# Raw blocks of the output set's two chainless products in eight tiles of the shared pool, and the residual's tiles behind the third group

## The chip, the cores and the metric

The kernel runs on one core of a Trainium2 chip. The metric is the device time of one execution in microseconds. TensorE (PE) multiplies, with its weight loads (PEld) beside it; VectorE (DVE), ScalarE (ACT) and GpSimd (POOL) do the rest of the arithmetic; SyncE (SP) and POOL issue most of the DMA transfers, and ACT a few. Each engine works through its own queue in order. All weights come from HBM in float32 and are used once.

## What is computed

One layer of a decoder trunk on 256 tokens of width 2048: a normalisation, one wide input projection, two token mixers side by side (gated linear attention and differential attention), their branch projections, a gated merge, an output projection, a normalisation and the residual. What matters here is the end:

```python
merged = jax.nn.sigmoid(m_a) * y_a + jax.nn.sigmoid(m_b) * y_b
out = merged @ w_out[l]
x = x + rmsnorm(out, post_norm_g[l])
```

`out` is 256 x 2048. Its columns are worked on in four groups of 512: o0, o1, o2 and o3. `x` on the right is the residual, which is needed only in the very last step.

## The kernel before

**Weights.** Every weight block of 128 x 1024 float32 (0.5 MB) is loaded raw, and then split into a rounded part `hi` (ACT, an `activation` with Copy) and a rest `lo` (DVE, a subtraction), since PE multiplies in a format of less precision: hi with both halves of the activations, lo with one. A unit of a regular group is such a block: twelve matmuls of 512 columns. `schedule()` lays down all units in one list of steps; `take` asks for the next one, and `emit_half` has by then written the load and the split of the four steps after it (`AHEAD`).

**Regular loads** are issued by SP (L311) into tiles tagged "raw", of which there are six. A load waits until the block six places before it in this ring has been split. `hi` and `lo` have three buffers each.

**Sets.** Eight pairs of groups ("sets", numbers 0 to 7) are multiplied as 2 x 2 blocks with seven products in place of eight. The seven products have four units each, of six matmuls (two 512-column halves of one raw block, L698). Set 7, called `OUT`, is the pair o0 and o1 of the output projection; its products come in the order p1, q7, p2, p5, q6, q3, p4. The weight operand of p1, p5, q7, q6 and p4 is a running sum or difference of raw blocks: it is kept in two "chains" of four tiles, to which POOL's accumulating DMAs add the next raw block (L232). A block that goes on the chain this way is a `refill`, issued two steps after the split that read the tile (`late`). The weight operands of **p2 and q3 are single raw blocks, not on a chain** (`chain_of` gives None). For set 7 these eight blocks are loaded by SP into the "raw" ring (L291, tile name raw_s), between the raw_o blocks of group o2.

**The last stretch.** y12 and y13 are the last two groups of the second branch projection (L497; raw_y). Then come the 28 units of set 7, spread between the 8 units of o2 (three or four before each), and then o3. `start_out` loads the chains' first blocks at the step of y12's first unit (`begin_out`). During y13 and set 7 the merged activations are turned: `mh` and `ml` (eight tiles) are the halves of the turned operand, `rawm` (four tiles) its unsplit form, from which `out_sum` makes the sums and `out_split` the pairs `msquare` for the products.

o3 is multiplied twice: once for the first 128 tokens while its blocks arrive, once for the other 128 from the kept splits (`keep`, seven of eight units; L479). Then follow the norm and the residual, and the output is stored (L1380, L1381). The second half of o3 and all that follows it work on blocks that are already split.

**Tiles.** Almost everything of 4 KB per partition lives in one pool of 34 tiles (`u(...)`): the chains, `mh`, `ml`, `rawm`, `msquare`, `keep`, the gains `pg`, the results `yg`, the residual `xres`. A tile is given out in the order in which the program first uses it, as soon as an older one has been read for the last time. `xres` (four tiles, 2 MB) is allocated and loaded by SP right after y13's loop, ahead of the o2 loop (L1349).

**Order.** A scheduler at compile time orders each engine's instructions by readiness and program order; what has no input to wait for, such as a load, moves to the front of its queue as far as its tile is free. Some instructions are pinned with `keep_in_program_order`. The loads of this change aren't.

Of the kernel before, what the change touches and what calls it, by code (L numbers as in the profile page):

```python
# [14 lines left out]
P = 128  # L15
# [114 lines left out]
OUT = 7  # L130
# [27 lines left out]
def chain_of(n, name):  # L158
    if n == OUT:
        return OUT_CHAINS.get(name)  # L160
    chain = PRODUCTS[name][1]
    return chain if chain is None else (chain + n) % 2
# [3 lines left out]
def hybrid_kernel(ctx: ExitStack, tc, xt, xn, preg, postg, w, w2, gkb, glag, lamv, diffg, ident_d, causal_d, lmask_d, out):  # L166
    nc = tc.nc
    pe, act, dve, pool, sp = nc.tensor, nc.scalar, nc.vector, nc.gpsimd, nc.sync
# [10 lines left out]
    def u(shape, name, dtype=F32):  # L179
        count[0] += 1  # L180
        return big.tile(shape, dtype, tag="u", name=f"{name}_{count[0]}")
# [9 lines left out]
    def ps(tag):  # L191
        count[0] += 1
        return psum.tile([P, 512], F32, tag="bank", name=f"{tag}_{count[0]}")
# [19 lines left out]
    chains = [[], []]  # L213
    begin = {steps.index((n, 0)) - 7 for n in (0, 1)}
    begin_out = steps.index(("y12", 0))
    set_steps = [step for step in steps if not isinstance(step[0], str)]

    def piece(key, q):
        size = sizes[key]
        at = begins[key] + q * size * P  # L220
        return w[at : at + P * size].rearrange("(p n) -> p n", p=P)

    refills = []
    plain = {}

    def block(n, name, unit, add=True, which=None):

        chain, (kh, g) = chain_of(n, name), which or PRODUCTS[name][2]
        src = piece(SETS[n][g], 2 * kh + unit // 2)[:, 1024 * (unit % 2) : 1024 * (unit % 2) + 1024]
        dst = chains[chain][unit] if chain is not None else plain[n, unit]  # L230
        if add:
            return pool.dma_start(dst, src, accum_op=ALU.add)  # L232
        return pool.dma_start(dst, src)  # L233

    def refill(i, n, name, unit, raw):

        late = lambda *args, **kw: refills.append((i + 2, args, kw))
        x, y = chains[n % 2][unit], chains[(n + 1) % 2][unit]
        if n == OUT:
            if name == "p1":  # L240
                late(n, "p5", unit)
            elif name == "q7":
                late(n, "q6", unit, which=(0, 0))
            elif name == "q6":
                late(n, "p4", unit)
        elif name == "p1":
            if n < 2:
                block(n, "q3", unit, add=False)
            late(n, "p5", unit)
        elif name == "p5" and n in MOVED:  # L250
            late(n, "q6", unit)
        elif name == "p5":
            dve.tensor_tensor(out=x, in0=x, in1=y, op=ALU.add)
            late(n, "q7", unit)
        elif name == "p2" and n in MOVED:
            late(n, "q7", unit)
        elif name == "p2":
            tc.keep_in_program_order(dve.tensor_tensor(out=x, in0=x, in1=raw, op=ALU.add))
        elif name == "q6" and n in MOVED:
            late(n, "p4", unit)  # L260
        elif name == "q6" and n not in FULL:
            plain[n, unit] = u([P, 1024], "plain")
            late(n, "p2", unit, add=False)
        elif name == "q7" and 0 < n < LAST:
            late(n + 1, "p1", unit, add=False)
        elif name == "p4" and 0 < n < LAST:
            late(n + 1, "q3", unit, add=False)
        while refills and refills[0][0] <= i:
            _, args, kw = refills.pop(0)
            block(*args, **kw)  # L270

    def emit_half():
        j = emitted[0]
        emitted[0] += 1
        key, unit = steps[j]
        if j in begin:
            start_sets()
        if j == begin_out:
            start_out()
        if isinstance(key, int):  # L280
            i = set_steps.index((key, unit))
            name, part = order_of(key)[unit // 4], unit % 4
            if key == 1 and part == 0 and unit < 16:
                fetch_square(PRODUCTS[order_of(key)[unit // 4 + 1]][0])
            chain, (kh, g) = chain_of(key, name), PRODUCTS[name][2]
            if (key, part) in plain and name == "p2":
                raw = plain.pop((key, part))
            elif chain is None:
                raw = wpool.tile([P, 1024], F32, tag="raw", name=f"raw_s{key}_{unit}", bufs=6)
                at = 1024 * (part % 2)  # L290
                sp.dma_start(raw, piece(SETS[key][g], 2 * kh + part // 2)[:, at : at + 1024])  # L291
            else:
                raw = chains[chain][part]
            hi_t = wpool.tile([P, 1024], F32R, tag="hi", name=f"hi_{j}")
            lo_t = wpool.tile([P, 1024], F32R, tag="lo", name=f"lo_{j}")
            act.activation(hi_t, raw, AF.Copy)  # L296
            dve.tensor_tensor(out=lo_t, in0=raw, in1=f32(hi_t), op=ALU.subtract)  # L297
            refill(i, key, name, part, raw)
            ready[j] = ((key, unit), hi_t, lo_t)
            return  # L300
        size = sizes[key]
        h = unit % 2
        src = piece(key, unit // 2)
        n = size // 2
        early = key == "v0"
        if j == 0:
            load_x(0, 1)
        if j == 2:
            load_x(2, 2)
        raw = wpool.tile([P, 1024], F32, tag="raw", name=f"raw_{key}_{unit}", bufs=6)  # L310
        i = sp.dma_start(raw[:, :n], src[:, n * h : n * h + n])  # L311
        if early:
            tc.keep_in_program_order(i)
            if j == 0:
                load_x(1, 1)
            for kt in X_LOADS[j // 2] if h else ():
                load_x(kt, 4)
        if early:
            prep_x(j)
            if 6 <= j < 14:  # L320
                square_x(j - 6)
        if key == "o3" and j + 1 < len(steps):
            hi_t, lo_t = u([P, 1024], "keep", F32R), u([P, 1024], "keep", F32R)
        else:
            hi_t = wpool.tile([P, 1024], F32R, tag="hi", name=f"hi_{j}")
            lo_t = wpool.tile([P, 1024], F32R, tag="lo", name=f"lo_{j}")
        fine = 2 if j == 0 else 1
        for i in range(fine):
            a, b = n * i // fine, n * (i + 1) // fine
            r = raw[:, a:b]  # L330
            act.activation(hi_t[:, a:b], r, AF.Copy)  # L331
            dve.tensor_tensor(out=lo_t[:, a:b], in0=r, in1=f32(hi_t[:, a:b]), op=ALU.subtract)  # L332
        ready[j] = (key, hi_t, lo_t)
# [325 lines left out]
    def start_sets():  # L659
        n = started[0]  # L660
        started[0] += 1
        while "squares" not in done:
            with tc.issue_after(latest[0]):
                next(operands, None)
        for c in range(2):
            chains[c][:] = [u([P, 1024], f"chain{c}") for _ in range(4)]
        for unit in range(4):
            tc.keep_in_program_order(block(n, "p1", unit, add=False))

    def start_out():  # L670
        for c in range(2):
            chains[c][:] = [u([P, 1024], f"chain{c}") for _ in range(4)]
        for unit in range(4):
            block(OUT, "p1", unit, add=False)
        for unit in range(4):
            block(OUT, "q7", unit, add=False, which=(1, 1))
        for unit in range(4):
            block(OUT, "q7", unit)
# [110 lines left out]
    def late():  # L789
        norm_row()  # L790
        yield
        lam()
        yield
# [102 lines left out]
    for hf in range(2):  # L896
        ts = {}
        for name in ("k", "q"):
            ts[name] = u([P, 2, 4, P], name)
            for c in range(4):  # L900
                o, o2 = (t.rearrange("p (b t) -> p b t", b=2) for t in channel_major(f"{name}{hf}{c}"))
                bc = rstd_bc.rearrange("p (b t) -> p b t", b=2)
                t = ts[name][:, :, c, :]
# [63 lines left out]
    for g in range(4):  # L967
# [5 lines left out]
        t = u([P, 2, 512], "ua")  # L973
# [198 lines left out]
    for g in range(4):  # L1172
# [3 lines left out]
        for b in range(2):  # L1176
            t = t2([P, 512], "part")
# [6 lines left out]
    first, both, raw = {}, {}, {}  # L1184
# [136 lines left out]
    for g in range(4):  # L1321
# [8 lines left out]
        for b in range(2):  # L1330
            t = both[g][:, b, :]
# [9 lines left out]
    pg = [u([P, 1024], "pg") for _ in range(2)]  # L1341
    for i in range(2):
        sp.dma_start(pg[i], postg[1024 * i : 1024 * i + 1024].partition_broadcast(P))
    xres = []
    for b in range(2):
        xres.append([])
        for i in range(2):
            t = u([P, 1024], "xres")
            sp.dma_start(t, xn[P * b : P * b + P, 1024 * i : 1024 * i + 1024])  # L1349
            xres[b].append(t)  # L1350
    yg = [[u([P, 1024], "yg") for _ in range(2)] for _ in range(2)]
    ssq = sm([P, 2, 5], "ossq", bufs=1)

# [4 lines left out]
    def gain(b, bank, lo, n):  # L1358
        c = slice(lo % 1024, lo % 1024 + n)
        dve.tensor_tensor(out=yg[b][lo // 1024][:, c], in0=bank, in1=pg[lo // 1024][:, c], op=ALU.mult)  # L1360
# [22 lines left out]
    for g in (2,):  # L1383
        banks = token_major(f"o{g}", 512, m_ops)
        for b in range(2):
            square(b, banks[b], 512, g)
            gain(b, banks[b], 512 * g, 512)
    bank = ps("mm")
    kept = []
    for q in range(8):  # L1390
# [78 lines left out]
```

## Time and profile before

| | us |
|---|---|
| median of three runs | 1107.38 (1106.74 to 1109.68) |
| the profiled execution | 1108.6 |
| its span in the trace | 1106.8 |
| PE busy | 1089.2 (98%) |
| DVE busy | 891.0 (81%) |
| ACT busy | 723.9 (65%) |
| POOL busy | 195.9 (18%) |
| mean DMA rate | 259 GB/s, 287.17 MB |

The span goes from the first to the last instruction of the trace. Busy time is the time in which an engine had an instruction in work; a matmul's recorded end is modelled, and since matmuls overlap, the distance between the starts of two of them tells more than the length of one: of 512 columns, they start about 0.227 us apart at the full clock. The chain of work that ended last is followed back from the last instruction, at each step to what released it. "Landing" of a transfer is the time from its issue to the arrival of all its bytes. In a group's row, `out<-in` are tile names without buffer numbers.

### The profile page before, as it was taken

To read this page: it belongs to the slowest core of one execution; us is meant where nothing else is said; L and a number is where in the kernel's file an instruction comes from. 1 tells how busy PE (TensorE), PEld (TensorE's weight loads), DVE (VectorE), ACT (ScalarE), POOL (GpSimd) and SP (SyncE) were. 2 spreads that over 40 slices of the span, in tenths; PEclk is the share of its full clock that TensorE was granted. 3 is DMA by queue.
4 is the path that set the end of the run, shared out by engine and by line. 5 is a ranking of instruction groups with operands and counts; after the bars stand their busy time and mean duration, and the time that the engine had idled before them with its cause. 6 is when DMAs were issued, how large, how long until landed. Compare 5 with 4: busy or idle time off the path is not lost.

```text
span 1106.8 us, 15617 instructions
## 1 busy us (share of the span) xinstructions
PE 1089.2 (98%) x5506; PEld 936.4 (85%) x5506; DVE 891.0 (81%) x1233; ACT 723.9 (65%) x1057; POOL 195.9 (18%) x299
## 2 busy tenths in 40 slices
PE   9999999999999999999999999999999999999977
PEld 9999888888888888888888888888888888888866
DVE  6787769997779698879888898887768688688964
ACT  7777455655656668777877777766566565537751
POOL 0112112000311201212221321222111222102100
PEclk9999999999999999999999999999999999999988
DMA  8889775748899758988899978999787999959962
GB/s 310 265 300 335 236 260 209 276 162 279 238 341 273 263 190 231 241 240 246 254 233 255 275 213 262 251 352 307 208 252 239 338 340 327 391 187 254 264 206 76
DMA packets 81966, 287.17 MB, mean 259 GB/s; under 512 B 9888, under 2 KB 10656, under 8 KB 81888
## 3 DMA queue, kind: packets, MB, share of 16 engines
q1 hardware_dynamic: 47792, 164.52, 41.7%
q0 software_dynamic: 33376, 120.60, 41.5%
q10 hardware_dynamic: 720, 1.06, 0.3%
q8 instruction: 43, 0.70, 0.2%
q14 instruction: 35, 0.29, 0.1%
HBM read 262.03 MB, written 24.12 MB: 259 GB/s over the span
## 4 chain that ended last, share of the span: by engine, by line
PE 92%; DVE 3%; DMA 2%; issue 2%; ACT 1%; DVEq 0%; POOLq 0%; POOL 0%; SPq 0%; ACTq 0%
PE mm L497 35%; PE set L698 26%; PE mm L518 15%; PE mm L520 8%; PE bg L497 2%; DMA raw_o<-in_w_dram 1%; PE bg L873 1%; PE bg L479 1%; PE bg L1012 1%; PE bg L1011 1%; DVE lo L297 1%; PE mm L479 0%; DVE lo L332 0%; PE bg L1037 0%; ACT hi L331 0%
## 5 line engine op out<-in xcount | busy, mean ns | idle before, releaser
L297 DVE TENSOR_TENSOR lo<-chain,hi 128x1024 fp32r<-128x1024 f32 x188 | 228.5, 1221 | 66.2 <-ACT hi L296 65.4
L296 ACT ACTIVATE hi<-chain 128x1024 fp32r<-128x1024 f32 x188 | 197.9, 1058 | 124.8 <-PE mm L497 48.8
L518 PE MATMUL mm<-xs,hi 128*128 128x512 f32 x768 | 197.7, 390 | 0.0
L518 PEld LDWEIGHTS mm<-xs,hi 128*128 128x128 f32 x768 | 143.3, 188 | 27.6
L497 PE MATMUL mm<-hi,xs 128*128 128x512 f32 (+2 forms) x640 | 151.7, 377 | 0.9 <-ACT hi L331 0.9
L232 POOL DMA_DIRECT2D chain<-in_w_dram x88 | 76.6, 871 | 358.0 <-DVE lo L297 213.9
L497 PEld LDWEIGHTS mm<-hi,xs 128*128 128x128 f32 x640 | 119.2, 189 | 16.5 <-ACT hi L331 1.2
L698 PE MATMUL set<-hi,square 128*128 128x512 f32 x448 | 121.7, 393 | 0.0
L520 PEld LDWEIGHTS mm<-xs,lo 128*128 128x128 f32 x768 | 104.7, 190 | 8.3 <-DVE lo L332 0.9
L520 PE MATMUL mm<-xs,lo 128*128 128x256 f32 x768 | 107.2, 282 | 0.5 <-DVE lo L332 0.5
L332 DVE TENSOR_TENSOR lo<-raw_y,hi 128x1024 fp32r<-128x1024 f32 x64 | 78.2, 1223 | 31.7 <-ACT hi L331 31.7
L331 ACT ACTIVATE hi<-raw_y 128x1024 fp32r<-128x1024 f32 x64 | 67.9, 1060 | 53.6 <-PE mm L497 34.2
L698 PEld LDWEIGHTS set<-hi,square 128*128 128x128 f32 x448 | 81.6, 189 | 14.6 <-ACT p L715 0.4
L698 PE MATMUL set<-hi,xs 128*128 128x512 f32 x336 | 91.0, 392 | 0.0
L497 PE MATMUL mm<-lo,xs 128*128 128x512 f32 (+2 forms) x320 | 81.9, 374 | 0.0
L698 PEld LDWEIGHTS set<-hi,xs 128*128 128x128 f32 x336 | 61.1, 189 | 10.5
L698 PE MATMUL set<-lo,square 128*128 128x512 f32 x224 | 69.5, 391 | 0.1
L497 PEld LDWEIGHTS mm<-lo,xs 128*128 128x128 f32 x320 | 60.0, 189 | 8.1 <-DVE lo L332 0.3
L233 POOL DMA_DIRECT2D chain<-in_w_dram x64 | 35.5, 571 | 147.0 <-DVE lo L297 114.7
L331 ACT ACTIVATE hi<-raw_ag 128x1024 fp32r<-128x1024 f32 x32 | 34.0, 1061 | 33.2 <-PE mm L497 19.3
L698 PE MATMUL set<-lo,xs 128*128 128x512 f32 x168 | 51.9, 390 | 0.0
L332 DVE TENSOR_TENSOR lo<-raw_v,hi 128x832 fp32r<-128x832 f32 (+2 forms) x41 | 40.9, 1009 | 12.9 <-ACT hi L331 12.8
(309 smaller groups left out, 2095.6 us busy)
## 6 DMA issues: line engine op xcount, KB each, us to landing
chain<-in_w_dram POOLq DMA_DIRECT2D x152, 512.0 KB, 8.8
raw_y<-in_w_dram SPq DMA_DIRECT2D x64, 512.0 KB, 7.0
raw_ag<-in_w_dram SPq DMA_DIRECT2D x32, 512.0 KB, 4.7
raw_dq<-in_w_dram SPq DMA_DIRECT2D x32, 512.0 KB, 6.0
raw_dk<-in_w_dram SPq DMA_DIRECT2D x32, 512.0 KB, 6.1
raw_v<-in_w_dram SPq DMA_DIRECT2D x32, 416.0 KB, 5.8
raw_s<-in_w_dram SPq DMA_DIRECT2D x20, 512.0 KB, 7.7
raw_k<-in_w_dram SPq DMA_DIRECT2D x16, 512.0 KB, 7.0
```

Source lines behind the costliest of these rows:

```text
L232: return pool.dma_start(dst, src, accum_op=ALU.add)
L233: return pool.dma_start(dst, src)
L296: act.activation(hi_t, raw, AF.Copy)
L297: dve.tensor_tensor(out=lo_t, in0=raw, in1=f32(hi_t), op=ALU.subtract)
L331: act.activation(hi_t[:, a:b], r, AF.Copy)
L332: dve.tensor_tensor(out=lo_t[:, a:b], in0=r, in1=f32(hi_t[:, a:b]), op=ALU.subtract)
L479: i = pe.matmul(out, lhs, rhs, start=first and n == 0, stop=last and n == len(pairs) - 1)
L497: i = pe.matmul(banks[g][b][:, :n], a[part][:, P * b : P * b + P], w[:, c : c + n], start=first, stop=last)
L518: i = pe.matmul(o, hi[:, c], x_pair(kt), start=kt == 0, stop=kt == KT - 1)
L520: i = pe.matmul(o[:, :S], lo[:, c], x_ops(kt)[0], start=False, stop=False)
L698: i = pe.matmul(bank, a[part], wt[:, 512 * j : 512 * j + 512], start=go, stop=end, skip_group_check=not first)
L873: pe.matmul(o, xk[:, P * c : P * c + P], xq.rearrange("p (b c t) -> p b c t", b=2, c=4)[:, :, c, :], start=i == 0, stop=i == 1)
```

## The change

For set 7, the eight raw blocks of p2 and q3 no longer go through the "raw" ring. Each has a tile of the shared pool:

- p2's four blocks are allocated and loaded at the step of y13's first unit (`begin_out + 8`), by POOL.
- q3's four blocks are allocated and loaded one by one as p1's four units are split (in `refill`), by SP.
- When the products come, `emit_half` finds the tile in `plain`, which is now keyed by the product's name too, and splits from it. The splits and matmuls are those of before.
- `xres` is allocated and loaded behind the o2 loop rather than ahead of it.

```diff
-    def block(n, name, unit, add=True, which=None):
+    def block(n, name, unit, add=True, which=None, queue=pool):
...
-        dst = chains[chain][unit] if chain is not None else plain[n, unit]
+        dst = chains[chain][unit] if chain is not None else plain[n, name, unit]
         if add:
             return pool.dma_start(dst, src, accum_op=ALU.add)
-        return pool.dma_start(dst, src)
+        return queue.dma_start(dst, src)
...
             if name == "p1":
                 late(n, "p5", unit)
+                plain[n, "q3", unit] = u([P, 1024], "plain")
+                block(n, "q3", unit, add=False, queue=sp)
...
-            plain[n, unit] = u([P, 1024], "plain")
+            plain[n, "p2", unit] = u([P, 1024], "plain")
             late(n, "p2", unit, add=False)
...
+        if j == begin_out + 8:
+            for n in range(4):
+                plain[OUT, "p2", n] = u([P, 1024], "plain")
+                block(OUT, "p2", n, add=False)
...
-            if (key, part) in plain and name == "p2":
-                raw = plain.pop((key, part))
+            if (key, name, part) in plain:
+                raw = plain.pop((key, name, part))
...
     pg = [u([P, 1024], "pg") for _ in range(2)]
     for i in range(2):
         sp.dma_start(pg[i], postg[1024 * i : 1024 * i + 1024].partition_broadcast(P))
-    xres = []
-    for b in range(2):
-        xres.append([])
-        for i in range(2):
-            t = u([P, 1024], "xres")
-            sp.dma_start(t, xn[P * b : P * b + P, 1024 * i : 1024 * i + 1024])
-            xres[b].append(t)
...
     for g in (2,):
         banks = token_major(f"o{g}", 512, m_ops)
         for b in range(2):
             square(b, banks[b], 512, g)
             gain(b, banks[b], 512 * g, 512)
+    xres = []
+    for b in range(2):
+        xres.append([])
+        for i in range(2):
+            t = u([P, 1024], "xres")
+            sp.dma_start(t, xn[P * b : P * b + P, 1024 * i : 1024 * i + 1024])
+            xres[b].append(t)
```

## The prediction, made before the change was run

> **What bounds the kernel now.** First the page: PE is busy throughout, and its slices fall off only at the end, where the change acts.
>
> ```profile
> PE 1089.2 (98%) x5506; PEld 936.4 (85%) x5506; DVE 891.0 (81%) x1233; ACT 723.9 (65%) x1057; POOL 195.9 (18%) x299
> PE   9999999999999999999999999999999999999977
> ```
>
> Next the table of stages over the last 150 us. Its columns are the stretch, its length, busy time of PE, PEld, DVE, ACT and POOL (with instruction counts), granted clock, DMA share, GB/s.
>
> ```profile
> 960.00:980.00 20.00, 20.00 (x90) 16.57 (x89) 16.71 (x15) 8.73 (x10) 0.00 (x0) 1.00 0.75 271
> 980.00:1000.00 20.00, 20.00 (x102) 16.80 (x101) 13.05 (x15) 8.91 (x11) 0.00 (x0) 1.00 0.56 178
> 1000.00:1020.00 20.00, 19.73 (x91) 16.09 (x90) 18.22 (x22) 16.25 (x22) 6.05 (x7) 1.00 0.96 270
> 1020.00:1040.00 20.00, 19.94 (x89) 16.19 (x87) 20.00 (x23) 16.19 (x19) 0.85 (x1) 1.00 1.05 288
> 1040.00:1060.00 20.00, 17.02 (x74) 13.76 (x74) 14.97 (x15) 9.57 (x12) 3.41 (x4) 1.00 0.99 254
> ```
>
> Until 1040 PE loses next to nothing. The DMA engines have room between 960 and 1000 (0.25 x 20 + 0.44 x 20 = 13.8 us) and none from 1000 to 1060. The chain of waits (start, length, what) then names the loss:
>
> ```profile
> 1049.43 11.31 DMA raw_o<-in_w_dram
> ...
> 1060.76 0.04 ACT keep L331
> ...
> 1061.72 1.05 ACT hi L331
> ...
> 1073.64 4.61 DMA raw_o<-in_w_dram
> ...
> 1078.27 1.07 ACT hi L331
> ...
> 1080.51 1.23 DVE keep L332
> ```
>
> A raw block of the last group (o3) takes 11.31 us to land. ACT, which works in order, stands at its split ("keep"); the split that PE needs, of the third group's seventh unit (o2), is queued behind it. PE's timeline prices it (start, length, instruction, idle before):
>
> ```profile
> 1056.40 0.61 PE L698 MATMUL set<-lo,msquare 128*128 128x512 f32 x2
> 1062.81 0.79 PE L497 MATMUL mm<-hi,mh 128*128 128x512 f32 x1 [5.80 <-ACT hi L331]
> 1067.66 0.40 PE L698 MATMUL set<-hi,mh 128*128 128x512 f32 x1
> 1073.13 0.39 PE L497 MATMUL mm<-hi,mh 128*128 128x512 f32 x1
> 1075.85 0.61 PE L479 MATMUL mm<-keep,mh 128*128 128x512 f32 x2
> 1081.29 0.99 PE L479 MATMUL mm<-keep,mh 128*128 128x512 f32 x2
> ```
>
> PE is idle for **5.80 us**. Then one unit (twelve matmuls) takes 1067.66 - 1062.81 = 4.85 us; the same work takes 1075.85 - 1073.13 = 2.72 us later, so **2.13 us** go to a slower clock, which the table in 5 us steps shows:
>
> ```profile
> 1055.00:1060.00 5.00, 2.02 (x9) 1.32 (x8) 0.21 (x1) 0.00 (x0) 0.00 (x0) 1.00 1.03 323
> 1060.00:1065.00 5.00, 2.19 (x5) 1.80 (x6) 2.21 (x2) 3.90 (x4) 0.00 (x0) 0.53 0.55 223
> ```
>
> The Trainium skill ("TensorE: Matmul & The Clock Gate", Part 1: The HAM clock gate) says that an idle window of about 3.4 us halves the clock. The trace agrees: idle from 1057.0, granted clock 0.53 in 1060 to 1065. By that rule a remaining wait below that length would cost itself alone.
>
> At 1081.29 a pair takes 0.99 in place of 0.61: **0.38 us**, again a split queued behind a late load (1073.64). All that the change can win is 5.80 + 2.13 + 0.38 = 8.31 us; PE's other work is untouched.
>
> **The change, part by part.** *The raw ring.* Loads of raw_o and of raw_s (the eight blocks) share six buffers, and a load is issued when the split of the load six places before it is done. SP's timeline (start, time from first to last, line, count):
>
> ```profile
> 999.67 0.33 SPq L291 DMA_DIRECT2D raw_s<-in_w_dram  x1
> ...
> 1001.08 2.58 SPq L1349 DMA_DIRECT2D xres<-in_xn_dram  x4
> ...
> 1028.37 7.81 SPq L291 DMA_DIRECT2D raw_s<-in_w_dram  x3
> 1043.33 30.64 SPq L311 DMA_DIRECT2D raw_o<-in_w_dram  x10
> ```
>
> The change takes eight of the 24 raw loads out of this ring. Then o2's seventh load follows the split of o2's first unit, and o3's first load that of o2's third:
>
> ```profile
> 1009.60 1.21 DVE L332 TENSOR_TENSOR lo<-raw_o,hi 128x1024 fp32r<-128x1024 f32 x1
> ...
> 1024.86 1.22 DVE L332 TENSOR_TENSOR lo<-raw_o,hi 128x1024 fp32r<-128x1024 f32 x1
> ```
>
> So they are issued near 1011 and 1026, not at 1043.33 and 1049.43. o2's fourth to sixth loads move ahead of 1000. That is what removes the 5.80 and the 2.13.
>
> *Price of a load.* 0.524 MB at 420 GB/s is 1.25 us (first row: plain loads). Where accumulating loads of the chains alternate with plain ones, two move in 1.05 MB / 276 GB/s = 3.80 us (second row): about 2.55 us for an accumulating load.
>
> ```profile
> 950.00:955.00 5.00, 5.00 (x24) 4.14 (x23) 3.37 (x3) 2.12 (x2) 2.17 (x5) 1.00 1.03 420
> 1030.00:1035.00 5.00, 5.00 (x24) 4.14 (x23) 5.00 (x6) 4.41 (x7) 0.00 (x0) 1.00 1.06 276
> ```
>
> *p2's four loads* go to POOL. The x tiles are read last at 957.0 (the tile view, first and last start at the row's end), so the pool has tiles then; POOL's next instruction comes only at 1002.67 after 45.27 us of idleness, so four issues (0.54 us each, as for "plain" before) hold up nothing there.
>
> ```profile
> L698 PE MATMUL set<-lo,xs x16: 389/389/389, 928.2 to 957.0; 128*128 128x512 f32 x16
> 1002.67 0.89 POOL L232 DMA_DIRECT2D chain<-in_w_dram  x1 [45.27 <-DVE lo L297]
> L233 POOL DMA_DIRECT2D plain<-in_w_dram x4: 527/542/618, 872.7 to 884.3; - x4
> ```
>
> On the DMA engines they take 4 x 1.25 = 5.0 us beside raw_y's loads. Those issued from 957 to 970 land after (minimum, median, maximum):
>
> ```profile
> DMA to landing us min/median/max: 3.6/6.4/7.1
> ```
>
> A raw_y buffer is needed again after six units of 2.72 us, less about 2.3 us of splitting: some 14 us after its issue. 7.1 + 5.0 = 12.1 fits. Cost 0, from 0 to 1 us if the cover is short.
>
> *q3's four loads* stay on SP, but with tiles of their own, near 975 to 1005 as tiles come free; until then each can hold the raw_y and raw_o loads behind it on SP. The xres loads, in the same position before, waited in total, how often, and longest (us):
>
> ```profile
> SPq L1349 <- PE mm L497: 1.0, 2, 0.6
> ```
>
> The six-deep ring hides that. Cost 0, at most 1 us. With p2's, and o2's three, less the three raw_s loads that already came before 1000, about seven loads, 9 us of DMA time, go into the 13.8 us of room.
>
> *xres* leaves 1001 to 1021 and comes behind o2: four plain loads, 5.0 us, on SP among o3's loads, beside the four accumulating loads of p4 (4 x 2.55 = 10.2 us). p4's issues (first and last start) and their landing (minimum, median, maximum):
>
> ```profile
> L232 POOL DMA_DIRECT2D chain<-in_w_dram x4: 847/851/857, 1041.3 to 1047.0; - x4
> ...
> DMA to landing us min/median/max: 5.5/9.5/13.5
> ```
>
> The last lands at 1060.5 at worst and is split by 1062.8; PE without the stall wants it at 1057.0 + 2.72 + 3 x 1.36 = 1063.8 (a unit of a product is six matmuls, 1.36 us). It fits by 1 us. xres itself is read only from 1089.0:
>
> ```profile
> L1380 DVE SCALAR_TENSOR_TENSOR yg<-yg,or,xres x8: 746/747/753, 1089.0 to 1102.2; 128x512 f32<-128x512 f32 x8
> ```
>
> *Tiles.* The turns write mh in 991.9 to 1018.3:
>
> ```profile
> L530 ACT ACTIVATE mh<-bg x8: 574/586/592, 991.9 to 1018.3; 128x512 fp32r<-128x512 f32 x8
> ```
>
> At the tightest point, near 1016, live are mh and ml 8, chains 8, rawm 4, pg 2, n7's sum and its pair 3, the eight new ones: 33 of 34, and a last gate and part. A wait for a tile there meets the last turn, at 1018, whose sum feeds p5, two products later. I take 0, from 0 to 2 us.
>
> *What is late next* is DVE. Its row for 1020 to 1040 says 20.00 of 20 us. From 1055 it has 14 splits of 1.23 us (the "keep" row above) and six products or sums of 0.67 us
>
> ```profile
> 1077.01 1.33 DVE L1360 TENSOR_TENSOR yg<-mm,pg 128x512 f32<-128x512 f32 x2
> ```
>
> or 21.2 us, ending at 1076.2; PE without the stall needs o3's last split at 1063.8 + 1.36 + 2.72 + 7 x 1.36 = 1077.4. It stays hidden by 1 us.
>
> **Sum.** 8.31 us less 0.4 for the thin margins (1 us at p4's last load and at DVE, the tiles) is 7.9. The profiled execution took 1108.6 us (span 1106.8): 1100.7. It lies 1.2 above the median of the runs, 1107.38; from that, **1099.5 us**.
>
> **Rivals.**
> *(a) xres puts o3's loads late again, in part.* SP and ACT are in order: xres lands behind p4's accumulations, o3's next loads behind xres, and a "keep" split queued too early holds ACT as at 1060.76. For: before, the xres loads landed after
>
> ```profile
> DMA to landing us min/median/max: 8.7/13.5/18.2
> ```
>
> and held the loads behind them. Against: the o3 loads concerned are needed from 1068, not 1057. Price: up to their 5.0 us of DMA time, on average 4: 1101.5 to 1105.5.
>
> *(b) The DMA is the bound, whichever queue.* The Trainium skill ("DMA: Bandwidth & Descriptors", Issuing engines are not separate DMA queues) says that loads from SP, ACT and POOL interleave on the same 16 DMA engines. The trace shows shares of 0.96, 1.05 and 0.99 from 1000 to 1060 with both queues open. If the new loads cannot start before 1000 (tiles come late), o3's last load lands at 1078 as before, and the wait moves to o3: 1107.4 within 2 us. Against: 13.8 us of room and tiles from 957.
>
> *(c) Slower: xres stands ahead of o3's last four loads.* If its tiles come only with the last chain (p4's splits, after 1062), SP waits there, and 5.0 us of xres precede o3's last load: landing 1073.64 + 4.61 + 5.0 = 1083.25. By the chain above PE resumes 3.5 us after that landing (1080.51 + 1.23, against 1078.25), so PE ends 5.0 us later than now: 1112.4. It decides from a last landing later than 1078.25. Against: by my count q3's tiles come free near 1050.
>
> **Chances.** Forecast 0.55 (1097.5 to 1101.5), (a) 0.22, (b) 0.11, (c) 0.12. A measurement tells about 0.3%, 3.3 us, from no change: faster means below 1104.1, slower above 1110.7. Faster 0.55 + 0.16 of (a) = 0.71; same 0.06 + 0.11 = 0.17; slower 0.12. The range takes the forecast, (a), and the nearest of (b): 1097.5 to 1106.0, with 0.8 in it.
>
> **What would show it.** Right: no idle PE near 1057, granted clock 1.00 from 1055 to 1070, raw_o's fourth load before 1000, plain's loads between 957 and 1005, o3's first landing before 1040, DMA share in 960 to 1000 up by 0.2, the tail after o3 unchanged. Wrong: PE waiting for an ACT split whose engine waits for raw_o after 1050 (a), plain's loads after 1000 (b), SP waiting at L1349's successor past 1060 (c), or PE waiting for raw_y near 965.

## The result, and the profile after

| | before | after |
|---|---|---|
| median, measured side by side (6 runs each) | 1107.36 (1106.53 to 1109.68) | 1099.64 (1098.68 to 1100.17) |
| the profiled execution | 1108.6 | 1100.08 |
| its span | 1106.8 | 1098.3 |

The ratio is 0.9926, 95% interval 0.9913 to 0.9939: 7.7 us faster; 1099.64 was measured where 1099.5 was predicted. In the listings of the changed kernel most lines have moved by six: the splits of raw blocks are L337 (ACT) and L338 (DVE), those of chains and of the early blocks L302 and L303, a group's matmuls L503, a set's L704, o3's L485, and SP's raw loads L317. The xres loads, which the change moves, are L1392; the loads of the early blocks ("plain") are L233.

The page after, its two lines on PE:

```profile
PE 1087.1 (99%) x5506; PEld 935.5 (85%) x5506; DVE 891.4 (81%) x1233; ACT 724.1 (66%) x1057; POOL 197.6 (18%) x303
...
PE   9999999999999999999999999999999999999997
```

PE's busy time fell by 2.1 us with the same 5506 matmuls, which is the size of the slow clock's loss; the rest of the 8.5 us of span was idle time. The table of stages, with the columns of the prediction's table:

```profile
960.00:980.00 20.00, 20.00 (x90) 16.57 (x89) 16.44 (x15) 8.99 (x10) 1.81 (x4) 1.00 0.98 392
980.00:1000.00 20.00, 20.00 (x102) 16.82 (x101) 13.05 (x15) 8.91 (x11) 0.00 (x0) 1.00 0.55 180
1000.00:1020.00 20.00, 19.76 (x91) 16.11 (x91) 18.38 (x22) 16.43 (x23) 6.04 (x7) 1.00 0.96 265
1020.00:1040.00 20.00, 20.00 (x89) 16.34 (x88) 20.00 (x23) 15.77 (x19) 0.85 (x1) 1.00 0.95 235
1040.00:1060.00 20.00, 20.00 (x89) 16.48 (x89) 19.72 (x22) 15.36 (x19) 3.41 (x4) 1.00 0.84 184
```

From 1040 to 1060 PE is busy for all 20 us (17.02 before) at clock 1.00, and the DMA share there fell from 0.99 to 0.84. The extra traffic ahead of 1000 shows in the first row alone: (392 - 271) GB/s x 20 us = 2.4 MB, between four and five blocks. PE has one wait left after 940 (who waits for what: us in total, times, longest):

```profile
PE bg L1218 <- DVE mgate L1339: 0.2, 1, 0.2
```

PE's timeline across the place of the old wait (start, length, instruction, idle before in brackets where there is any):

```profile
1056.56 0.62 PE L704 MATMUL set<-lo,msquare 128*128 128x512 f32 x2
1057.02 0.39 PE L503 MATMUL mm<-hi,mh 128*128 128x512 f32 x1
...
1059.73 0.39 PE L704 MATMUL set<-hi,mh 128*128 128x512 f32 x1
...
1067.89 0.61 PE L485 MATMUL mm<-keep,mh 128*128 128x512 f32 x2
```

ACT's timeline, before and then after:

```profile
1060.76 1.06 ACT L331 ACTIVATE keep<-raw_o 128x1024 fp32r<-128x1024 f32 x1 [7.58 <-DMA raw_o<-in_w_dram]
```

```profile
1053.24 1.05 ACT L337 ACTIVATE keep<-raw_o 128x1024 fp32r<-128x1024 f32 x1
1054.19 1.04 ACT L337 ACTIVATE hi<-raw_o 128x1024 fp32r<-128x1024 f32 x1
```

ACT still takes the split of o3's first block ("keep") ahead of that of o2's seventh unit ("hi"), but now the block lies there and neither row has an idle time, where ACT stood 7.58 us before. PE goes from the set to o2's seventh unit without a gap at 1057.02, that unit takes 1059.73 - 1057.02 = 2.71 us, and o3 begins at 1067.89 in place of 1075.85: 7.96 us earlier, against 5.80 + 2.13 = 7.93 in the prediction. From o3's first matmul to the end of the span it is 30.41 us (1098.3 - 1067.89), 0.54 us less than before (1106.8 - 1075.85 = 30.95). SP's timeline:

```profile
983.77 16.50 SPq L317 DMA_DIRECT2D raw_o<-in_w_dram  x6
1000.32 1.52 SPq L233 DMA_DIRECT2D plain<-in_w_dram  x3
1001.95 2.00 SPq L1349 DMA_DIRECT2D pg<-in_postg_dram  x2
1004.04 0.40 SPq L233 DMA_DIRECT2D plain<-in_w_dram  x1
1011.14 54.95 SPq L317 DMA_DIRECT2D raw_o<-in_w_dram  x10
1066.14 1.86 SPq L1392 DMA_DIRECT2D xres<-in_xn_dram  x4
```

o2's first six loads are now all issued by 1000.3. Its seventh follows at 1011.14, and o3's first, the third of the run of ten, in SP's timeline from 1026 to 1027:

```profile
1026.22 0.33 SPq L317 DMA_DIRECT2D raw_o<-in_w_dram  x1
```

These are the 1011 and 1026 of the prediction. o3's first block lands 8.9 us later, at 1035.1, long before ACT comes to it at 1053.24. The xres loads went to the very end, behind all of o3's.

### The profile page after: what moved, and what is told of

It reads as the page before. It is cut to its first block, busy times and chain, and to the rows that moved or that the text cites. A ratio compares the mean times of both kernels' runs of the same rounds, so it can differ in the third digit from the quotient of the medians.

```text
span 1098.3 us, 15622 instructions
## 1 busy us (share of the span) xinstructions
PE 1087.1 (99%) x5506; PEld 935.5 (85%) x5506; DVE 891.4 (81%) x1233; ACT 724.1 (66%) x1057; POOL 197.6 (18%) x303
## 4 chain that ended last, share of the span: by engine, by line
PE 94%; DVE 3%; issue 1%; DMA 0%; ACT 0%; DVEq 0%; POOLq 0%; POOL 0%; SPq 0%; ACTq 0%
PE mm L503 36%; PE set L704 27%; PE mm L524 15%; PE mm L526 8%; PE bg L503 2%; PE mm L485 1%; PE bg L879 1%; PE bg L485 1%; PE bg L1018 1%; PE bg L1017 1%; DVE lo L338 1%; DVE chain L260 1%; PE bg L1043 0%; DVE lo L303 0%; PE bg L1218 0%
## 5 line engine op out<-in xcount | busy, mean ns | idle before, releaser
L303 DVE TENSOR_TENSOR lo<-chain,hi 128x1024 fp32r<-128x1024 f32 x188 | 228.5, 1222 | 65.8 <-ACT hi L302 63.9
L302 ACT ACTIVATE hi<-chain 128x1024 fp32r<-128x1024 f32 x188 | 198.1, 1058 | 125.0 <-PE mm L503 48.9
L503 PE MATMUL mm<-hi,xs 128*128 128x512 f32 (+2 forms) x640 | 151.8, 377 | 0.6 <-ACT hi L337 0.6
L503 PEld LDWEIGHTS mm<-hi,xs 128*128 128x128 f32 x640 | 119.4, 189 | 16.2 <-ACT hi L337 0.9
L704 PE MATMUL set<-hi,square 128*128 128x512 f32 x448 | 121.7, 393 | 0.0
L338 DVE TENSOR_TENSOR lo<-raw_y,hi 128x1024 fp32r<-128x1024 f32 x64 | 78.3, 1223 | 31.7 <-ACT hi L337 31.7
L337 ACT ACTIVATE hi<-raw_y 128x1024 fp32r<-128x1024 f32 x64 | 67.9, 1060 | 53.5 <-PE mm L503 34.1
L704 PEld LDWEIGHTS set<-hi,square 128*128 128x128 f32 x448 | 81.6, 188 | 14.7 <-ACT p L721 0.4
L704 PE MATMUL set<-hi,xs 128*128 128x512 f32 x336 | 91.0, 392 | 0.0
L503 PE MATMUL mm<-lo,xs 128*128 128x512 f32 (+2 forms) x320 | 82.1, 374 | 0.0
L704 PEld LDWEIGHTS set<-hi,xs 128*128 128x128 f32 x336 | 61.1, 189 | 10.5
L704 PE MATMUL set<-lo,square 128*128 128x512 f32 x224 | 69.5, 391 | 0.1
L503 PEld LDWEIGHTS mm<-lo,xs 128*128 128x128 f32 x320 | 60.0, 189 | 8.1 <-DVE lo L338 0.3
L233 POOL DMA_DIRECT2D chain<-in_w_dram x64 | 35.5, 565 | 147.1 <-DVE lo L303 111.8
L337 ACT ACTIVATE hi<-raw_ag 128x1024 fp32r<-128x1024 f32 x32 | 34.0, 1062 | 33.2 <-PE mm L503 19.4
L704 PE MATMUL set<-lo,xs 128*128 128x512 f32 x168 | 51.8, 390 | 0.0
L338 DVE TENSOR_TENSOR lo<-raw_v,hi 128x832 fp32r<-128x832 f32 (+2 forms) x41 | 40.3, 995 | 12.7 <-ACT hi L337 12.5
```

The source lines that it names most:

```text
L233: return queue.dma_start(dst, src)
L503: i = pe.matmul(banks[g][b][:, :n], a[part][:, P * b : P * b + P], w[:, c : c + n], start=first, stop=last)
L704: i = pe.matmul(bank, a[part], wt[:, 512 * j : 512 * j + 512], start=go, stop=end, skip_group_check=not first)
```

## The experiments

The theory was the prediction's: PE waited since ACT, in order, stood at the split of o3's first block, which landed late; and it landed late since its buffer of the ring came free late. The rivals: the full DMA engines bound the stretch whatever the order; and the gain is due to the xres loads leaving it. Each run is compared with runs of the kernel before on the same chip. Line numbers differ by a few from run to run; the tile names tell which instruction it is.

| run | median, us | before, us | ratio (95%) |
|---|---|---|---|
| 1 xres_alone | 1107.40 | 1107.75 | 0.9997 (0.9987 to 1.0006) |
| 2 p2_alone | 1107.41 | 1107.75 | 0.9994 (0.9985 to 1.0004) |
| 3 q3_alone | 1112.83 | 1107.75 | 1.0044 (1.0029 to 1.0059) |
| 4 before_keeps_pinned | 1100.31 | 1107.75 | 0.9933 (0.9917 to 0.9950) |
| 5 both_xres_ahead | 1100.77 | 1107.97 | 0.9933 (0.9918 to 0.9948) |
| 6 q3_last_two | 1105.66 | 1107.97 | 0.9980 (0.9971 to 0.9989) |
| 7 q3_last_one | 1104.63 | 1107.97 | 0.9969 (0.9956 to 0.9981) |
| 8 xres_in_o3 | 1100.11 | 1107.97 | 0.9925 (0.9911 to 0.9938) |
| 9 q3_xres_behind | 1099.97 | 1108.13 | 0.9927 (0.9911 to 0.9943) |
| 10 o3_first_early | 1101.29 | 1108.13 | 0.9937 (0.9923 to 0.9951) |
| 11 after_keeps_pinned | 1098.60 | 1108.13 | 0.9914 (0.9900 to 0.9927) |

**One part at a time (1, 2, 3).** Run 1 is the kernel before with only the xres loads moved behind o2, where the change has them:

```diff
         sp.dma_start(pg[i], postg[1024 * i : 1024 * i + 1024].partition_broadcast(P))
-    xres = []
-    for b in range(2):
...
             gain(b, banks[b], 512 * g, 512)
+    xres = []
+    for b in range(2):
...
```

> The kernel before, with only the residual's loads moved behind the third group. Theory (ring and ACT order): the raw ring still holds all 24 loads, so o3's first load is still issued after the split of o2's sixth unit, near 1049.4, still lands near 1060 and still holds ACT; about 1107.4 us, within 1 us, PE idle 5 to 6 us near 1057. Rival (contention: what counts is how many bytes move between 1000 and 1060): four loads, 5.0 us of DMA time, leave that stretch; about 1103 us.

Run 2 is the kernel before with only p2's four blocks loaded early, by POOL (the lookup in `plain` is that of the change):

```diff
+        if j == begin_out + 8:
+            for n in range(4):
+                plain[OUT, "p2", n] = u([P, 1024], "plain")
+                block(OUT, "p2", n, add=False)
```

> The kernel before, with only p2's four blocks in tiles of the pool, loaded early by POOL; q3 through the ring, the residual ahead of the third group. Theory: the load six places before o3's first is still that of o2's sixth unit, so o3's first load is issued near 1049.4 as before; about 1107.4 us, within 1 us. Rival (contention): one load less after 1000, three raw_o loads earlier; about 1103 to 1105 us.

Run 3 is the kernel before with only q3's four blocks in tiles of their own. xres stays where it was before, as it does in runs 6 and 7, which are variants of this one:

```diff
             if name == "p1":
                 late(n, "p5", unit)
+                plain[n, "q3", unit] = u([P, 1024], "plain")
+                block(n, "q3", unit, add=False, queue=sp)
```

> The kernel before, with only q3's four blocks in tiles of the pool; p2 through the ring, the residual ahead of the third group. Theory: the load six places before o3's first is now that of o2's third unit, split near 1026, so the whole gain is there: 1099.6 us, within 1 us, no idle PE near 1057, granted clock 1.00 from 1055 to 1070. Rival (contention): four loads out of the stretch, the residual still in it; about 1103 us.

For neither xres nor p2 alone is a difference shown. PE's longest wait after 940 in run 1, then in run 2:

```profile
PE mm L497 <- ACT hi L331: 5.0, 1, 5.0
```

```profile
PE mm L501 <- ACT hi L335: 4.9, 1, 4.9
```

The old wait stands in both, a little shorter than the 5.80 us. In run 2 SP's timeline says why four loads fewer in the ring don't help:

```profile
1009.36 0.33 SPq L315 DMA_DIRECT2D raw_o<-in_w_dram  x1
1017.64 17.02 SPq L295 DMA_DIRECT2D raw_s<-in_w_dram  x3
1041.82 29.30 SPq L315 DMA_DIRECT2D raw_o<-in_w_dram  x10
```

The last run of ten begins with o2's last two, and o3's first load is its third. The six places ahead of it are those two, the three raw_s (q3's blocks) and the raw_o of 1009.36. So its buffer comes free with the split of that raw_o, o2's sixth unit, just as in the kernel before. Of the eight blocks only three of q3's stand in between; p2's were never among these six.

Run 3 does take q3's out, and was slower than before, where 1099.6 was expected: a miss. Its waits of PE, then SP's timeline, then the longest transfer of its chain (start, length):

```profile
PE set L700 <- ACT hi L298: 10.1, 1, 10.1
```

```profile
1000.12 1.58 SPq L233 DMA_DIRECT2D plain<-in_w_dram  x3
1001.80 1.03 SPq L1345 DMA_DIRECT2D pg<-in_postg_dram  x2
1002.93 2.46 SPq L1351 DMA_DIRECT2D xres<-in_xn_dram  x4
1006.57 0.33 SPq L233 DMA_DIRECT2D plain<-in_w_dram  x1
1010.94 0.33 SPq L293 DMA_DIRECT2D raw_s<-in_w_dram  x1
```

```profile
1010.94 28.79 DMA raw_s<-in_w_dram
```

The old wait is gone, but q3's four loads (plain), pg's two and xres's four are now one run of ten loads issued on SP within 7 us (a convoy, in what follows), and the next load behind it is p2's last raw block. It lands 28.79 us after its issue, and PE waits 10.1 us for its split. A wait for o3 was exchanged for a longer one for p2. The expectation had also counted wrongly: with p2 still in the ring, six places ahead of o3's first load stands p2's last block, not o2's third unit, so o3's first load was issued at 1042.18, behind that late split, and not near 1026.

**The order on ACT alone (4).** No load is moved; ACT's splits of o3 are held in program order, behind all of o2's and the set's:

```diff
-            act.activation(hi_t[:, a:b], r, AF.Copy)
+            split = act.activation(hi_t[:, a:b], r, AF.Copy)
+            if key == "o3":
+                tc.keep_in_program_order(split)
```

> The kernel before, all loads as they were; only ACT's splits of o3's blocks are pinned in program order, behind the split of o2's eighth unit. Theory: o2's seventh block had landed long before 1057, and the 5.80 us were ACT standing at o3's first block; with the order changed they go, and the slow clock with them, though o3's first load still takes about 11 us: 1099.6 to 1101 us. Rival (the late loads themselves bound the end): 1107 us within 1 us, the wait only moves to o3's first matmul near 1068.

The gain comes whole, as far as the intervals tell. A row of its table of stages, and its ACT timeline:

```profile
1040.00:1060.00 20.00, 20.00 (x90) 16.54 (x89) 19.61 (x20) 13.78 (x17) 3.41 (x4) 1.00 0.99 252
```

```profile
1052.69 1.06 ACT L331 ACTIVATE hi<-raw_o 128x1024 fp32r<-128x1024 f32 x1 [0.70 <-PE set L700]
...
1061.82 2.94 ACT L331 ACTIVATE keep<-raw_o 128x1024 fp32r<-128x1024 f32 x3
```

The DMA engines carry what they carried before (0.99 and 252 GB/s; 0.99 and 254 before), and PE has no wait above 0.3 us after 940: o2's seventh split runs at 1052.69, o3's first at 1061.82, and o3 needs nothing earlier. So the full DMA engines were not the bound, and the late block cost time only through ACT's order: the split of o3's first block stood ahead of one that PE wanted sooner.

**Where xres stands (5, 8).** Run 5 is the changed kernel with the xres loads back ahead of the o2 loop; run 8 is the changed kernel with them pinned between o3's fourth and fifth loads, to bring about what rivals (a) and (c) feared:

```diff
+        if key == "o3" and unit >= 4:
+            tc.keep_in_program_order(i)
...
-            sp.dma_start(t, xn[P * b : P * b + P, 1024 * i : 1024 * i + 1024])
+            tc.keep_in_program_order(sp.dma_start(t, xn[P * b : P * b + P, 1024 * i : 1024 * i + 1024]))
```

> The changed kernel with the residual's loads back ahead of the third group: twelve tiles more in use at once near 1016 than at the end. Theory (ring and ACT order): the ring is as free as in the changed kernel; 1099.6 us within 1 us, waits for tiles hidden. Rival (tiles: the residual had to make room): 37 tiles wanted of 34 near 1016, the last turn waits, PE idle 1 to 4 us between 1010 and 1045; 1101 to 1104 us.

> The changed kernel with the residual's four loads pinned on SP between o3's fourth and fifth load (in the changed kernel they came behind all of o3). Theory: o3's last four loads land up to 5 us later, but PE has the second half of o3's first four units to do meanwhile; 1099.6 us within 1 us. Rival (a) and (c) of the prediction: ACT or PE waits for o3's later blocks; 1101 to 1105 us, PE idle 1 to 5 us after 1068.

No difference from the changed kernel is shown for either. Run 5 lies 1.17 us above the expected 1099.6, just outside its band, with one wait of 0.8 us in o3; PE does not wait near 1016, where the rival feared for tiles. SP's timeline of run 8 from 1040 on:

```profile
1042.30 6.45 SPq L317 DMA_DIRECT2D raw_o<-in_w_dram  x2
1048.80 2.23 SPq L1394 DMA_DIRECT2D xres<-in_xn_dram  x4
1055.36 9.56 SPq L317 DMA_DIRECT2D raw_o<-in_w_dram  x4
```

PE's only wait after 940 in run 8 is one of 0.2 us.

**How many of q3's blocks (6, 7).** The kernel before with only the last two, or the last one, of q3's blocks in tiles of their own:

```diff
+                if unit in (2, 3):
+                    plain[n, "q3", unit] = u([P, 1024], "plain")
+                    block(n, "q3", unit, add=False, queue=sp)
```

> The kernel before, with only the last two of q3's blocks in tiles of the pool. Theory: six places before o3's first load stands o2's fifth unit, split by 1043.4; o3's first load is issued there and lands near 1050, before ACT comes to it near 1053: the whole gain, 1099.6 us within 1 us. Rival (contention): half of q3's share, about 1105 us.

> The kernel before, with only the last of q3's blocks in a tile of the pool. Theory: six places before o3's first load stands q3's first block, split by 1048.0; o3's first load is issued 1.4 us earlier than before and lands near 1058, so PE idles about 3 us near 1057 and not 5.8. If so short a pause leaves the clock at 1.00, the time is about 1102.6 us; if the clock still drops, about 1104.7 us. Rival (contention): an eighth of the loads, about 1106 us.

Run 6 missed for the reason of run 3, by a convoy of eight: PE waits 3.45 us for the split of p2's last block. In run 7 PE does not wait for p2's block, and the old wait is only shortened, to 3.05 us, since o3's first load follows a block one place earlier. The clock stayed at 1.00, for which 1102.6 had been expected; that 1104.63 agrees with the 1104.7 expected for a dropped clock is chance. What the expectation left out are further waits of PE for DVE, 0.7 us in o3 and 0.5 us at the set. PE's row at each wait, with the clock around it:

```profile
1034.03 0.80 PE L701 MATMUL set<-hi,mh 128*128 128x512 f32 x1 [3.45 <-ACT hi L299]
```

```profile
1030.00:1035.00 5.00, 1.55 (x5) 0.99 (x4) 1.34 (x2) 2.08 (x3) 0.00 (x0) 0.86 1.07 278
1035.00:1040.00 5.00, 5.00 (x19) 4.05 (x18) 4.52 (x5) 4.86 (x7) 0.00 (x0) 0.80 1.03 311
```

```profile
1058.99 0.50 PE L500 MATMUL mm<-hi,mh 128*128 128x512 f32 x1 [3.05 <-ACT hi L334]
```

```profile
1055.00:1060.00 5.00, 1.95 (x9) 1.29 (x8) 1.03 (x1) 3.07 (x4) 0.00 (x0) 1.00 1.01 338
1060.00:1065.00 5.00, 5.00 (x23) 4.11 (x22) 5.00 (x7) 3.88 (x6) 0.00 (x0) 1.00 0.45 150
```

**Is it the convoy? (9)** Run 3 again, with the xres loads behind o2, so that the convoy has six loads:

> q3's four blocks in tiles of their own, and xres behind o2; p2's four blocks stay in the raw ring. Theory (q3 alone was slower because its four loads, the two of pg and the four of xres stand on SP as one run of ten ahead of p2's last raw block, which was issued at 1010.94 and landed at 1039.73, and PE waited 10.06 us for its split): without xres four loads of 3.8 us, 15.3 us, leave the run, so p2's last block lands near 1024.5, ahead of the 1030.9 at which PE wants it; o3's first block lands before 1053, so PE waits nowhere for more than 1 us: 1100 within 1.5. Rival (q3's own four loads are what puts p2's block late, four more loads in 1000 to 1025 are too many wherever xres stands): the block lands after 1033 and PE waits 3 us or more: 1104 or more.

It is: run 9 has the whole gain with p2's four blocks left in the ring. The landing of raw_s blocks (minimum, median, maximum over the kernel) in run 3 and in run 9:

```profile
DMA to landing us min/median/max: 3.8/7.0/28.8
```

```profile
DMA to landing us min/median/max: 3.6/6.5/14.1
```

Four loads fewer ahead bring the worst landing down by 14.7 us, where about 15 (four of 3.8) had been worked out, and PE has no wait above 0.3 us after 940. The worst landing is that of p2's last block in both. The other traces have the same block, issued 4 to 7 us after the convoy's last load, and its landing goes with the number of loads in the convoy, whichever they are:

| | before | run 9 | run 7 | run 6 | run 3 |
|---|---|---|---|---|---|
| loads of pg, xres and q3 ahead | 6 | 6 | 7 | 8 | 10 |
| landing of p2's last block, us | 14.2 | 14.1 | 17.9 | 22.2 | 28.8 |

From six loads to ten, each further one costs 3.7 us on average.

**One block (10).** The kernel before with a single load moved:

```diff
+        if j == begin_out + 8:
+            first = plain["o3"] = u([P, 1024], "plain")
+            pool.dma_start(first, piece("o3", 0)[:, :1024])
...
+        if key == "o3" and unit == 0:
+            raw = plain.pop("o3")
...
```

> The kernel before with a single block taken out of the ring: o3's first, in one tile of the shared pool, loaded by POOL at y13's first unit; the eight blocks of p2 and q3 and xres stay where they were, and ACT's order with its split ahead of that of o2's seventh unit stays too. Theory (the wait is only that ACT stands at the split of o3's first block, which lands late): PE runs on at 1057, no wait over 1 us before 1070; o3's second block, landing near 1060, comes in ACT's queue behind o2's seventh unit and is not in the way: 1100.3 within 1.5. Rival (the eight early loads are needed, because the DMA engines are full from 1000 to 1060 and only moves the wait to the next block of o3): PE waits 3 us or more near 1060: 1104 to 1107.4.

One tile and one early load give nearly all of it. ACT's timeline, then PE's two waits in o3:

```profile
1052.72 1.04 ACT L337 ACTIVATE keep<-plain 128x1024 fp32r<-128x1024 f32 x1
1053.67 1.05 ACT L337 ACTIVATE hi<-raw_o 128x1024 fp32r<-128x1024 f32 x1
...
1061.14 1.06 ACT L337 ACTIVATE keep<-raw_o 128x1024 fp32r<-128x1024 f32 x1 [1.52 <-DMA raw_o<-in_w_dram]
```

```profile
1073.78 0.51 PE L485 MATMUL mm<-keep,mh 128*128 128x512 f32 x1 [0.37 <-ACT keep L337]
...
1075.23 0.50 PE L485 MATMUL mm<-keep,mh 128*128 128x512 f32 x1 [0.94 <-DVE keep L338]
```

ACT has the same order as before and passes o3's first block at 1052.72. The rest of o3 still comes late: ACT stands 1.52 us at its second block, and PE waits 0.37 + 0.94 = 1.31 us in o3. That much of the rival (the wait moves on) is true.

**Both remedies (11).** The changed kernel with ACT's splits of o3 in program order, by the edit of run 4:

> The changed kernel with ACT's splits of o3 held in program order, so that none stands ahead of a split of o2. Theory (after the change o3's first block has landed long before ACT comes to its split, so the order no longer matters): 1099.6 within 1, no difference from the changed kernel. Rival (the early split of o3's first block still costs, or saves, time on ACT): more than 1.5 us from the changed kernel.

1098.60 is the lowest median of all, but its interval (0.9900 to 0.9927) overlaps the changed kernel's (0.9913 to 0.9939), and the two were not timed side by side: no difference is shown.

## Why the prediction was right, step by step

- **The wait and its price** held. The 5.80 and the 2.13 us went (7.96 found at o3's start). The wait of 0.38 us is gone too, though not for the reason given: o3's last blocks still land late (see below). The sum was 7.9, the medians differ by 7.72. That they agree so closely is partly luck: the runs of the changed kernel alone span 1.5 us, and nothing shows the 0.4 that was taken off for thin margins (the profiled spans differ by 8.5).
- **The cause** held, and run 4 sharpens it: it was ACT's order together with the late block, and mending either of the two suffices. The DMA engines stayed as full in run 4, so rival (b) falls, although one of its signs did appear: q3's four loads came after 1000.
- **"Taking eight of 24 loads out of the ring"** was right in its result: o3's first load came at 1026.22. It was too broad in its reason. In the kernel before only q3's last three stand in the six places ahead of o3's first load, and moving p2's four alone frees nothing (run 2). p2's four are needed for something that the prediction had not seen: left in the ring, the last of them stands behind the convoy that q3's loads form with pg and xres (run 3), unless xres is moved (run 9). So p2's early loads and the xres move are each a cover for the other: beside q3's loads, with either the change works (runs 5 and 9), with neither it costs 5 us (run 3).
- **q3's loads** were put at 975 to 1005, spread as tiles come free. They came in one run from 1000.32 to 1004.44, and the DMA share from 980 to 1000 didn't move (0.56 and 0.55). Of the seven loads that were to go into the room ahead of 1000, four to five came, and the share from 960 to 1000 rose by 0.11 on average and not by 0.2. That step failed at no cost only because nothing urgent stood behind them: the next load on SP, o2's seventh at 1011.14, took 15.4 us to land and was split only at 1054.19. "Cost 0, at most 1 us" held for the whole change; alone, q3's four loads made PE wait 10.1 us.
- **xres among o3's loads** didn't happen: they were issued behind all of them. So the changed kernel itself tests neither the margin of 1 us at p4's last load nor rivals (a) and (c). Run 8 does: there they were issued from 1048.80 to 1051.03, just behind p4's (1040.3 to 1046.8), and it still cost nothing that can be measured. The rivals were priced by PE's order in the kernel before, but that order changed, in run 8 and in the changed kernel, whose PE timeline has:

```profile
1073.34 0.40 PE L485 MATMUL mm<-keep,mh 128*128 128x256 f32 x2
...
1076.92 0.40 PE L485 MATMUL mm<-keep,mh 128*128 128x512 f32 x1
```

- **DVE late next**, hidden by 1 us: another thing was late, and another one covered it. DVE begins its last split of a kept o3 block at 1077.0, later than the prediction's sum (its end at 1076.2):

```profile
L338 DVE TENSOR_TENSOR keep<-raw_o,keep x7: 1212/1216/1220, 1060.0 to 1077.0; 128x1024 fp32r<-128x1024 f32 x7
```

  It was not the amount of its work that made it late. DVE stood 3.00 us for ACT, and ACT 2.69 us for a load of o3:

```profile
1072.42 1.06 ACT L337 ACTIVATE hi<-raw_o 128x1024 fp32r<-128x1024 f32 x1 [2.69 <-DMA raw_o<-in_w_dram]
```

```profile
1073.51 1.22 DVE L338 TENSOR_TENSOR lo<-raw_o,hi 128x1024 fp32r<-128x1024 f32 x1 [3.00 <-ACT hi L337]
```

  PE does not wait for it, since from 1073.34 to 1076.92 it multiplies the second half (128x256) of blocks that are already split, and then goes back to the first. The two halves of o3 are a store of work that covers late blocks for 3.6 us, but only where the scheduler has put it so. In the kernel before and in runs 2, 3, 5, 6, 7 and 10 PE finishes the first half before it begins the second, and in each of them it loses 0.3 to 1.3 us in o3 by late splits. In the changed kernel and in runs 1, 8, 9 and 11, all with xres behind o2, it takes some of the second half early and has no such wait. Run 4 has none either, with xres ahead and half a microsecond of the second half taken early.

  So the xres move may be worth some tenths of a microsecond in this way; the medians are too coarse to show it, and why the scheduler's order changed with it stays open.

## What to carry to other kernels

When an engine waits for a split or a copy, look at what its in-order helper was doing: a scheduler may have queued an instruction for a later block ahead, and the cure can be one added pin rather than eight tiles. When loads are taken out of a ring, count which ones stand between the late load and its buffer; taking out the others does not free it sooner. And a group of loads that isn't urgent, and becomes ready at one moment, is a convoy for the next urgent load on that queue: price it by the landing interval of that stretch, and test each half of a change alone before calling one superfluous.

## What the runs showed of the hardware

- The length of idleness that costs clock was bracketed by two rows: after 3.05 us without a matmul (run 7) the granted clock stayed at 1.00, after 3.45 us (run 6) it fell, to 0.86 and 0.80 in the two 5 us steps around. The Trainium skill ("TensorE: Matmul & The Clock Gate", Part 1: The HAM clock gate) gives a window of about 3.4 us; the traces agree.
- A load of 0.5 MB on SP took 28.79 us to land when ten others had been issued on the same queue ahead of it and POOL's accumulating loads ran beside them, and 14.1 us with six ahead (run 9). The load's own size was the same. Whether the queue or the engines' total load sets this was not separated.
- DMA engines that are full did not by themselves hold up PE: run 4 has a DMA share of 1.05 from 1020 to 1040 and of 0.99 from 1040 to 1060, and no wait of PE above 0.3 us there. It depends on which load comes late: in run 3, with the same share of 1.05 from 1020 to 1040, PE waited 10.1 us.
